# Two-model kernel: conv taps in portions of four and an output product that accumulates over both halves in shared PSUM banks

## The chip, the cores and the metric

The kernel runs on one core of a Trainium2 chip. The metric is device microseconds (us) of one execution; lower is better. The engines are called by the names of the profile: PE (TensorE, matmuls; PEld its weight loads), DVE (VectorE), ACT (ScalarE), POOL (GpSimd) and SP (SyncE, whose queue issues most transfers).

## The reference, cut to what matters

The program computes two models one after the other. The change touches the first one alone: two layers over 256 tokens of width 1024. Each layer projects a normed input to many pieces, mixes tokens in three ways (a causal depthwise convolution with 31 taps, a pooling mixer, sparse attention), gates each, and multiplies the three joined results by `w_out`.

```python
for i in range(DEPTH):                      # DEPTH = 2
    n = rmsnorm(h, norm_g[i])
    z = n @ w_in[i] + b_in[i]
    (c_val, c_glu, c_gate, p_in, p_gate, q, k, v, a_gate, qi, ki, wi) = jnp.split(z, cut, axis=-1)
    ya = conv_module(c_val, c_glu, ...) * jax.nn.silu(c_gate)   # 31 taps, layernorm, silu, 1x1
    yb = pool_mixer(p_in, ...) * jax.nn.silu(p_gate)
    yc = sparse_attention(q, k, v, qi, ki, wi) * jax.nn.silu(a_gate)
    h = h + jnp.concatenate([ya, yb, yc], axis=-1) @ w_out[i]
    h = h + (p[i] @ ple_w[i]) * jax.nn.sigmoid(h @ ple_gate_w[i])
return rmsnorm(h, final_norm_g)
```

## The kernel before

Activations lie transposed: 128 features on the partitions, 256 tokens along the row, so a tensor of width 1024 is eight tiles of 128x256. Each operand of a large product is split into a high and a low half (`split`, `unit`), and one product is three matmuls: high by high, high by low, low by high (`mm3`). A weight unit of 128x1024 is loaded by SP into `raw`, its high half is copied by ACT and its low half is a subtraction on DVE (`hl<-raw,hl`, line 449). In the notes below, "the split" of a weight unit is this subtraction. An output tile with all eight input tiles takes 24 matmuls (`mtile`).

A layer of the first model runs like this: the norm; the tiles for the convolution, indexer, q, k and v; then eight **gate tiles** (`silu` of the gates, 24 matmuls each, one weight unit each); then the output product with `w_out` in two halves `g = 0, 1`, each over four of its eight input tiles (`WO_ORDER`). Each half has eight output tiles of 12 matmuls, and each is added to `h` on DVE (128x256, called `x` in traces). In the second half `h` is split again for the next product. After that the side input's product and its gate follow.

Convolution, pooling, indexer and attention are generators (`conv1`, `pool1`, `index1`, `attn1`). They run in the shadow of the tiles: `tick(budget)` is called behind a tile and lets tasks issue until the costs that they yield have used up the budget (1500 where nothing is given). From the gates on the tasks take turns. `conv1` issues one `scalar_tensor_tensor` of 128x256 (`acc<-u,sp,acc`, stt for short) for each filter position and each of two channel halves, 60 in a layer; each of these instructions is called a tap here. It yields `CONVY` = 900 after every two of them. Behind the taps come its norm (`acc,o`, `csq`, `clr` in the trace) and its 1x1 product (`csq,sw`). Attention's matmuls are named `kr,qr`, `aL` (transposes) and `aPT,v`. `flush()` between the halves lets all tasks run out, since the second half's input tiles are the convolution's and the last heads' results.

The order within each engine is then settled by a scheduler, and all engines run their own stream in order. PSUM banks are handed out by tag: three for `mm`, four for `ax` (tasks), one for `ada`.

Of the kernel before, what the change touches and what calls it, by code (L numbers as in the profile page):

```python
# [12 lines left out]
ALU = mybir.AluOpType  # L13
# [4 lines left out]
T = 256  # L18
KT = 8
# [3 lines left out]
FIRST = 2  # L23
PAIR_PACE = 2.2
DOWN_PACE = 2.5
CONVY = 900
INNER = 650
INNER_K = (1, 3, 5)
R_TICK, NQ_TICK, SC_TICK = 650, 900, 1000
# [75 lines left out]
WO_ORDER = (2, 3, 4, 5, 6, 7, 0, 1)  # L105
# [247 lines left out]
class Prog:  # L353
# [209 lines left out]
        return ps  # L563


    def ftile(s, x, keep=False):
        w = s.raw0.pop(0) if s.raw0 else s.rawunit()
        ps = s.bank("mm")
        for k in range(KT):
            if keep:  # L570
                s.warm(KEEP, 256)
            s.mm(ps[:, :T], w[:, k * 128 : k * 128 + 128], x[:, k], k == 0, k == KT - 1)
        return ps
# [164 lines left out]
    def layer1(s, i):  # L738
# [9 lines left out]
        h = s.h  # L748
# [8 lines left out]
        gh = s.gh  # L757
        rs = s.t([128, T], "rs", 1)

        def norm():  # L760
            R = s.spread(s.rstd_cols(s.st[0]["ps"][:, 0:2], 2, 1.0 / D), 2)
            s.a(rs, R[:, :T], AF.Copy)
            for k in range(KT):
                n = s.t([128, T], "nf", 2, pool=s.sm)
                s.tt(n, gh[:, k], rs, ALU.mult)
                s.split(s.xx[:, 1, 0, k], s.xx[:, 1, 1, k], n)

        tile_no = [-1]
        raws = [s.ftile(gh, i == 0 and j == 0) for j in range(FIRST)]
        norm()  # L770

        def wtile():
            tile_no[0] += 1
            if tile_no[0] not in PLAIN:
                return s.mtile(T, T)
            ps = raws.pop(0) if raws else s.ftile(gh)
            y = s.t([128, T], "yc", 2)
            s.tt(y, ps[:, :T], rs, ALU.mult)
            return y
# [5 lines left out]
        def bias():  # L785
            j = bi[0]
            bi[0] += 1
            return P["b"][:, j : j + 1], H["b"][:, j : j + 1]
# [6 lines left out]
        for j in range(2):  # L795
            ps = wtile()
# [7 lines left out]
        for j in range(2):  # L804
            ps = wtile()
# [11 lines left out]
        ps = wtile()  # L817
# [5 lines left out]
        for tt in range(2):  # L823
            ps = s.bank("mm")
            for k in range(KT):
                o = (k % 3) * 260
# [4 lines left out]
        for j in range(2):  # L831
            ps = wtile()
# [10 lines left out]
        for nme in ("q", "k"):  # L843
            raw = s.t([128, 4, T], nme + "r", 1)
            for j in range(4):
                ps = wtile()
# [8 lines left out]
        for uu in range(4):  # L855
            hl = s.unit()
            for tt in range(2):
                for kk in range(2):
                    k = uu * 2 + kk
# [19 lines left out]
        for j in range(8):  # L879
            ps = s.mtile(T, T)  # L880
            b, hb = bias()
            zh = s.t([128, T], "zh", 2)
            th = s.t([128, T], "th", 2)
            s.a(th, ps[:, :T], AF.Tanh, bias=hb, scale=0.5)
            s.a(zh, ps[:, :T], AF.Identity, bias=hb, scale=0.5)
            s.stt(sil[:, j], th, 1.0, zh, ALU.add, ALU.mult)
            st8[GATES[j]] = sil[:, j]
            if i == DEPTH - 1 and j == RCTX:
                ps = s.spread(rc, 2)
                s.a(s.rctx, ps[:, :T], AF.Copy)  # L890
            s.tick()
        s.pace = PACE[3]
        s.pool_share = 0.0
        s.until(st8, "pool")
        s.until(st8, ("att", 1))


        for g in range(2):
            if g:
                s.turns = False  # L900
                s.flush()
            for m in range(KT):
                if m % 2 == 0:
                    hl = s.unit()
                ps = s.mtile(0, T, hl, WO_ORDER[4 * g : 4 * g + 4], m % 2 * 4)
                s.tt(h[:, m], h[:, m], ps[:, :T], ALU.add)
                if g:
                    s.split(s.xx[:, 1, 0, m], s.xx[:, 1, 1, m], h[:, m])
                s.tick()
        s.pace = PACE[4]  # L910
        if i < DEPTH - 1:
            s.spn = s.small1(i + 1)
# [10 lines left out]
        for m in range(KT):  # L923
            pe = s.bank()
            for k in range(2):
                o = (m % 4) * 256 + k * 128
# [3 lines left out]
            ps = s.mtile(T, T)  # L930
# [4 lines left out]
            e = nc.gpsimd if SQP[0] else None  # L935
            s.sumsq_add(st[0], h[:, m], 2, m == 0, m == KT - 1, eng=e)
            out, g = (h, P["fin"]) if lastl else (s.gh, s.spn["g"])
# [13 lines left out]
    def conv1(s, i, P, H, u, cat, st8):  # L951
        nc = s.nc
        acc = s.t([128, 2, T], "acc", 1)
        for j in range(2):
            s.ts(acc[:, j], u[:, j, 0:T], P["dw"][:, j * CONV_K : j * CONV_K + 1], ALU.mult,
                 P["dwb"][:, j : j + 1], ALU.add)
        for k in range(1, CONV_K):
            for j in range(2):
                s.stt(acc[:, j], u[:, j, k : k + T], P["dw"][:, j * CONV_K + k : j * CONV_K + k + 1], acc[:, j],
                      ALU.mult, ALU.add)  # L960
            yield CONVY
        while "late" not in st8:
            yield None
        o256 = s.t([128, 128], "o256", 1)
        s.ts(o256, s.ones, 1.0 / 256, ALU.mult)
        ps = s.bank()
        for j in range(2):
            s.mm(ps[:, :T], o256, acc[:, j], j == 0, j == 1)
        for j in range(2):
            s.tt(acc[:, j], acc[:, j], ps[:, :T], ALU.subtract)  # L970
        yield CSTEP
        sq = s.t([128, 2, T], "csq", 1)
        s.a(sq, acc, AF.Square)
        st = s.bank()
        for tt in range(2):
            for j in range(2):
                s.mm(st[:, tt : tt + 1], sq[:, j, tt * 128 : tt * 128 + 128], s.ones[:, 0:1], j == 0, j == 1)
        r = s.rstd_cols(st[:, 0:2], 2, 1.0 / 256, "cl")
        yield CSTEP
        R = s.spread(r, 2)  # L980
        for j in range(2):
            s.tt(acc[:, j], acc[:, j], R[:, :T], ALU.mult)
            th = s.t([128, T], "th", 2)
            s.a(th, acc[:, j], AF.Tanh, bias=H["lnb"][:, j : j + 1], scale=H["lng"][:, j : j + 1])
            s.a(sq[:, j], acc[:, j], AF.Identity, bias=H["lnb"][:, j : j + 1], scale=H["lng"][:, j : j + 1])
            s.stt(sq[:, j], th, 1.0, sq[:, j], ALU.add, ALU.mult)
            yield 700
        while ("c", 1) not in st8:
            yield None
        pw = P["pw"].rearrange("p (k f) -> p k f", k=2)  # L990
        for m in range(2):
            ps = s.bank()
            for j in range(2):
                s.mm(ps[:, :T], pw[:, j, m * 128 : m * 128 + 128], sq[:, j], j == 0, j == 1)
            s.stt(acc[:, m], ps[:, :T], P["pwb"][:, m : m + 1], st8["c", m], ALU.add, ALU.mult)
            s.split(cat[0][:, m], cat[1][:, m], acc[:, m])
            yield 700
        st8["conv"] = True
# [776 lines left out]
```

## Time and profile before

| What | Value |
|---|---|
| Time, median of 3 runs | 1443.52 us (1440.94 to 1445.94) |
| The profiled execution | 1444.92 us |
| Its span in the trace | 1443.1 us |
| Mean granted clock of TensorE | 0.98 |
| Busy: PE, DVE, ACT, POOL | 1388.4, 1134.6, 671.9, 68.4 us |

The profiled execution's time is a little more than its span, which runs from the first to the last event that the trace holds. Busy times overlap. The granted clock is the share of TensorE's full speed that it was given. In the traces an idle entry `[0.98 <-ACT xx L414]` says that the engine stood idle for 0.98 us before the instruction, and which instruction ended the wait.

### The profile page before, as it was taken

To read this page: it belongs to the slowest core of one execution; us is meant where nothing else is said; L and a number is where in the kernel's file an instruction comes from. 1 tells how busy PE (TensorE), PEld (TensorE's weight loads), DVE (VectorE), ACT (ScalarE), POOL (GpSimd) and SP (SyncE) were. 2 spreads that over 40 slices of the span, in tenths; PEclk is the share of its full clock that TensorE was granted. 3 is DMA by queue.
4 is the path that set the end of the run, shared out by engine and by line. 5 is a ranking of instruction groups with operands and counts; after the bars stand their busy time and mean duration, and the time that the engine had idled before them with its cause. 6 is when DMAs were issued, how large, how long until landed. Compare 5 with 4: busy or idle time off the path is not lost.

```text
span 1443.1 us, 25346 instructions
## 1 busy us (share of the span) xinstructions
PE 1388.4 (96%) x9914; PEld 1188.0 (82%) x9914; DVE 1134.6 (79%) x2430; ACT 671.9 (47%) x1234; POOL 68.4 (5%) x92
## 2 busy tenths in 40 slices
PE   8999899998999999998999999999899999999997
PEld 7878899788978777678888888888788887999997
DVE  6998679997879666897788877888678556798794
ACT  4446555465753241545443312443145346565562
POOL 0000000000200001003000000001200000100001
PEclk9999899998999998999999999999999999999998
DMA  7973356334543432332444564557732232366662
GB/s 263 330 250 118 103 170 201 125 104 130 194 148 116 132 100 73 117 114 89 133 144 132 160 191 146 174 177 251 229 115 89 89 97 88 116 212 197 183 198 74
DMA packets 63903, 219.03 MB, mean 152 GB/s; under 512 B 7270, under 2 KB 12328, under 8 KB 63528
## 3 DMA queue, kind: packets, MB, share of 16 engines
q1 hardware_dynamic: 58368, 209.22, 45.8%
q10 hardware_dynamic: 5416, 8.20, 1.7%
q8 instruction: 78, 1.28, 0.4%
q14 instruction: 41, 0.34, 0.1%
HBM read 216.34 MB, written 1.05 MB: 151 GB/s over the span
## 4 chain that ended last, share of the span: by engine, by line
PE 73%; DVE 11%; issue 6%; DMA 4%; ACT 3%; POOL 2%; ACTq 0%; POOLq 0%; DVEq 0%; SPq 0%
PE mm L388 20%; PE mm L389 20%; PE mm L390 19%; PE ax L385 9%; DVE hl L449 3%; DMA wada<-in_wadaT_dram 2%; PE mm L385 1%; DMA raw<-in_units_dram 1%; PE ax L1728 1%; PE ada L385 1%; POOL sqa L537 1%; DVE xx L396 1%; DVE wada L683 1%; DMA crow<-in_crow_dram 1%; ACT hl L441 1%
## 5 line engine op out<-in xcount | busy, mean ns | idle before, releaser
L388 PE MATMUL mm<-xx,hl 128*128 128x256 f32 (+1 forms) x1720 | 557.5, 326 | 5.5 <-ACT xx L414 2.0
L390 PE MATMUL mm<-xx,hl 128*128 128x256 f32 (+1 forms) x1720 | 547.1, 319 | 1.6 <-DVE hl L449 1.5
L389 PE MATMUL mm<-xx,hl 128*128 128x256 f32 (+1 forms) x1720 | 547.6, 319 | 0.0
L441 ACT ACTIVATE hl<-raw 128x1024 fp32r<-128x1024 f32 x286 | 301.3, 1055 | 186.8 <-PE mm L390 152.4
L449 DVE TENSOR_TENSOR hl<-raw,hl 128x1024 fp32r<-128x1024 f32 x286 | 348.9, 1221 | 49.3 <-ACT hl L441 47.6
L388 PEld LDWEIGHTS mm<-xx,hl 128*128 128x128 f32 x1720 | 325.6, 190 | 51.8 <-issue 17.9
L390 PEld LDWEIGHTS mm<-xx,hl 128*128 128x128 f32 x1720 | 325.9, 190 | 30.6 <-DVE hl L449 3.2
L389 PEld LDWEIGHTS mm<-xx,hl 128*128 128x128 f32 x1720 | 326.5, 190 | 28.4 <-issue 4.9
L396 DVE SCALAR_TENSOR_TENSOR y<-mm,sp,y 128x255 f32<-128x255 f32 (+1 forms) x184 | 109.0, 595 | 30.9 <-ACT y L409 29.6
L389 PE MATMUL mm<-hid,hl 128*128 128x256 f32 (+1 forms) x374 | 124.2, 332 | 0.0
L388 PE MATMUL mm<-hid,hl 128*128 128x256 f32 (+1 forms) x374 | 124.2, 332 | 0.0
L390 PE MATMUL mm<-hid,hl 128*128 128x256 f32 (+1 forms) x374 | 124.1, 332 | 0.0
L683 DVE CUSTOM_DVE_ANT_0 wada<-wada,crow,sp 128x1024 f32<-128x1024 f32 x80 | 102.9, 1292 | 13.6 <-DMA wada<-in_wadaT_dram 13.2
L409 ACT ACTIVATE y<-mm,sp 128x256 f32<-128x256 f32 (+1 forms) x92 | 60.5, 658 | 97.9 <-PE mm L390 97.8
L390 PEld LDWEIGHTS mm<-hid,hl 128*128 128x128 f32 x374 | 71.9, 192 | 7.1
L388 PEld LDWEIGHTS mm<-hid,hl 128*128 128x128 f32 x374 | 71.8, 192 | 7.1
L389 PEld LDWEIGHTS mm<-hid,hl 128*128 128x128 f32 x374 | 71.8, 192 | 7.1
L389 PE MATMUL mm<-hl,xx 128*128 128x416 f32 (+3 forms) x192 | 65.9, 346 | 2.5 <-DVE hl L449 2.5
L396 DVE SCALAR_TENSOR_TENSOR x<-mm,mod,x 128x256 f32<-128x256 f32 x96 | 43.6, 479 | 30.2 <-PE mm L390 30.1
L537 POOL TENSOR_TENSOR sqa<-sqa,sq 128x256 f32<-128x256 f32 x36 | 35.3, 987 | 675.7 <-ACT sq L409 674.8
L388 PE MATMUL mm<-hl,xx 128*128 128x416 f32 (+3 forms) x192 | 65.9, 349 | 0.2 <-ACT hl L441 0.2
L390 PE MATMUL mm<-hl,xx 128*128 128x416 f32 (+3 forms) x192 | 65.6, 344 | 0.0
(278 smaller groups left out, 1691.0 us busy)
## 6 DMA issues: line engine op xcount, KB each, us to landing
raw<-in_units_dram SPq DMA_DIRECT2D x296, 512.0 KB, 3.8
wada<-in_wadaT_dram SPq DMA_DIRECT2D x80, 512.0 KB, 3.5
wada<-in_wada_dram SPq DMA_DIRECT2D x16, 512.0 KB, 6.2
nab<-in_nab_dram ACTq DMA_DIRECT2D x12, 192.0 KB, 3.4
crow<-in_crow_dram SPq DMA_DIRECT2D x2, 1024.0 KB, 7.4
x<-in_xT_dram SPq DMA_DIRECT2D x4, 256.0 KB, 5.9
x<-in_ctxT_dram ACTq DMA_DIRECT2D x1, 1024.0 KB, 11.9
c<-in_c_dram ACTq DMA_DIRECT2D x1, 928.0 KB, 5.9
```

Of the source, the lines that this page charges most:

```text
L385: return s.nc.tensor.matmul(out, lhsT, rhs, start=start, stop=stop, **kw)
L388: s.nc.tensor.matmul(out, l[0], r[0], start=start, stop=False)
L389: s.nc.tensor.matmul(out, l[0], r[1], start=False, stop=False)
L390: s.nc.tensor.matmul(out, l[1], r[0], start=False, stop=stop)
L396: s.nc.vector.scalar_tensor_tensor(out, a, sc, b, op0, op1)
L409: s.nc.scalar.activation(out, in_, func, bias=bias, scale=scale)
L441: a = nc.scalar.activation(hl[:, 0], raw, AF.Copy)
L449: b = nc.vector.tensor_sub(hl[:, 1], raw, hl[:, 0].bitcast(F32))
L537: (eng or s.nc.vector).tensor_tensor(st["acc"], st["acc"], sq, ALU.add)
L683: s.pin(nc.vector.tensor_tensor_reduce(out=w, in0=w, in1=c[:, j], scale=1.0, scalar=bias[:, m : m + 1], op0=ALU.mult, op1=ALU.add, accum_o ...
L1728: nc.tensor.transpose(pt[:, kt * 128 : kt * 128 + 128], L[j][:, kt * 128 : kt * 128 + 128], s.ident)
```

## The change

Four edits, all in the first model. The taps are issued four at a time, and such a portion costs 1300. A gate tile's tick has a budget of 2800. The norm works on pairs of tiles (128x512). The output product keeps its sums in four PSUM banks (three `mm`, one `ada`) over both halves: a bank holds a pair of output tiles side by side, the first half (`g = 0`) only accumulates, and in the second half one addition of 128x2x256 and one split of 128x512 follow per pair. Ticks are left in the first half only. Lines behind the edits move by 1 to 18 (the split of weight units is line 450, the matmuls of the output product are line 386).

```diff
-CONVY = 900
+CONVY = 1300
+GATE_TICK = 2800
...
+    def part(s, out, hl, ks, off, g):
+        for q, k in enumerate(ks):
+            o = (q + off) * 128
+
+            s_, e_ = not g and not off and q == 0, bool(g) and bool(off) and q == len(ks) - 1
+            r = [s.mv(e, k, 0, T) for e in range(2)]
+            kw = dict(skip_group_check=True)
+            s.mm(out, hl[:, 0, o : o + 128], r[0], s_, False, **kw)
+            s.mm(out, hl[:, 0, o : o + 128], r[1], False, False, **kw)
+            s.mm(out, hl[:, 1, o : o + 128], r[0], False, e_, **kw)
...
-            for k in range(KT):
-                n = s.t([128, T], "nf", 2, pool=s.sm)
-                s.tt(n, gh[:, k], rs, ALU.mult)
-                s.split(s.xx[:, 1, 0, k], s.xx[:, 1, 1, k], n)
+            for k in range(0, KT, 2):
+                n = s.t([128, 2, T], "nh", 2)
+                s.tt(n, gh[:, k : k + 2], rs.unsqueeze(1).to_broadcast([128, 2, T]), ALU.mult)
+                s.split(s.xx[:, 1, 0, k : k + 2], s.xx[:, 1, 1, k : k + 2], n)
...
-            s.tick()
+            s.tick(GATE_TICK)
...
+        wo = [s.bank("mm" if b < 3 else "ada") for b in range(4)]
         for g in range(2):
             if g:
                 s.turns = False
                 s.flush()
-            for m in range(KT):
-                if m % 2 == 0:
-                    hl = s.unit()
-                ps = s.mtile(0, T, hl, WO_ORDER[4 * g : 4 * g + 4], m % 2 * 4)
-                s.tt(h[:, m], h[:, m], ps[:, :T], ALU.add)
+            for m in range(0, KT, 2):
+                hl, ps = s.unit(), wo[m // 2]
+                for d in range(2):
+                    s.part(ps[:, d * T : d * T + T], hl, WO_ORDER[4 * g : 4 * g + 4], d * 4, g)
+                    if not g:
+                        s.tick()
                 if g:
-                    s.split(s.xx[:, 1, 0, m], s.xx[:, 1, 1, m], h[:, m])
-                s.tick()
+                    hm = h[:, m : m + 2]
+                    s.tt(hm, hm, ps.rearrange("p (k t) -> p k t", k=2), ALU.add)
+                    s.split(s.xx[:, 1, 0, m : m + 2], s.xx[:, 1, 1, m : m + 2], hm)
...
-            yield CONVY
+            if k % 2 == 0:
+                yield CONVY
```

Three places show how the order on the engines moves, all in layer 0. The first is PE between the two halves of the output product before; `mm_1716`, `mm_1732` and `mm_1753` are tiles of the second half.

```order
L385 MATMUL ax_1662<-c_82,csq_1660 128x1 x4
L385 MATMUL ax_1671<-c_82,clr_1669 128x128 x2
L385 MATMUL ax_1684<-csq_1660,sw_102 128x256
L385 MATMUL ax_1690<-csq_1660,sw_102 128x256
L1104 MATMUL ax_1696<-c_82,aL_1593 128x128
L385 MATMUL ax_1684<-csq_1660,sw_102 128x256
L385 MATMUL ax_1690<-csq_1660,sw_102 128x256
L1104 MATMUL ax_1696<-c_82,aL_1593 128x128 x3
L385 MATMUL ax_1624<-aPT_1701,v_816 64x128 x4
L388 MATMUL mm_1716<-xx,hl_1713 128x256
L388 MATMUL mm_1732<-xx,hl_1713 128x256
L388 MATMUL mm_1753<-xx,hl_1750 128x256
```

After the change PE's stream at the end of the first half reads as follows; `mm_1534`, `mm_1535`, `mm_1536` and `ada_1537` are the four shared banks.

```order
L1122 MATMUL ax_1569<-c_82,aL_1529 128x128 x2
L386 MATMUL mm_1535<-xx,hl_1598 128x256
L1122 MATMUL ax_1569<-c_82,aL_1529 128x128 x2
L386 MATMUL mm_1535<-xx,hl_1598 128x256 x9
L386 MATMUL ax_1560<-aPT_1574,v_808 64x128 x4
L386 MATMUL mm_1535<-xx,hl_1598 128x256 x14
L386 MATMUL mm_1536<-xx,hl_1627 128x256 x24
L386 MATMUL ada_1537<-xx,hl_1656 128x256 x24
L386 MATMUL mm_1534<-xx,hl_1685 128x256 x24
L386 MATMUL mm_1535<-xx,hl_1717 128x256 x24
L386 MATMUL mm_1536<-xx,hl_1749 128x256 x24
L386 MATMUL ada_1537<-xx,hl_1781 128x256 x24
```

The last attention matmuls (`aPT`) and transposes (`aL`) stood between the halves and stand inside the first half now; 62 matmuls of the product lie between the last of them and the second half, and the conv norm's matmuls (`csq`, `clr`) have moved from here to the gate tiles.

The second place is DVE from the end of the v tiles to the split for a gate tile, before; `hl_1069` belongs to gate tile 3, `v_816` is the sum for v.

```order
L449 TENSOR_TENSOR hl_1069<-raw_1067,hl_1069 128x1024
L1052 MATCH_REPLACE iwk_757<-im_758,iwk_757 128x256
L405 TENSOR_TENSOR v_816<-mm_817,tokb_109 128x512
L1051 MAX im_758<-iwk_757 128x8
L405 TENSOR_TENSOR mod_452<-ax_930,sp_249 128x4x2
L1052 MATCH_REPLACE iwk_757<-im_758,iwk_757 128x256
L405 TENSOR_TENSOR mod_452<-ax_930,sp_249 128x4x2
L405 TENSOR_TENSOR imk_873<-iwk_757,isc_699 128x256
L405 TENSOR_TENSOR v_816<-mm_818,tokb_109 128x512
L402 TENSOR_SCALAR imk_873<-imk_873 128x256
L396 SCALAR_TENSOR_TENSOR acc_390<-u_206,sp_80,acc_390 128x256 x2
L449 TENSOR_TENSOR hl_1123<-raw_1121,hl_1123 128x1024
```

After the change the stretch that ends with the split for gate tile 1 (`hl_945`) reads like this.

```order
L397 SCALAR_TENSOR_TENSOR acc_374<-u_190,sp_80,acc_374 128x256
L1070 MATCH_REPLACE iwk_749<-im_750,iwk_749 128x256
L397 SCALAR_TENSOR_TENSOR acc_374<-u_190,sp_80,acc_374 128x256
L406 TENSOR_TENSOR imk_865<-iwk_749,isc_691 128x256
L397 SCALAR_TENSOR_TENSOR acc_374<-u_190,sp_80,acc_374 128x256
L403 TENSOR_SCALAR imk_865<-imk_865 128x256
L397 SCALAR_TENSOR_TENSOR acc_374<-u_190,sp_80,acc_374 128x256
L406 TENSOR_TENSOR mod_444<-ax_926,sp_233 128x4x2 x2
L397 SCALAR_TENSOR_TENSOR acc_374<-u_190,sp_80,acc_374 128x256 x4
L406 TENSOR_TENSOR v_808<-mm_809,tokb_109 128x512
L406 TENSOR_TENSOR v_808<-mm_810,tokb_109 128x512
L450 TENSOR_TENSOR hl_945<-raw_943,hl_945 128x1024
```

Before, the first gates' splits stood ahead of the additions to v, with few taps between; now eight taps and both additions to v come ahead of the first gate's split. By the split of gate tile 5, 28 of the layer's 60 taps have been issued before, and all 60 after, in either layer.

The third place is DVE in the second half of the output product, before.

```order
L405 TENSOR_TENSOR x_70<-x_70,mm_1716 128x256
L415 TENSOR_TENSOR xx<-x_70,xx 128x256
L405 TENSOR_TENSOR x_70<-x_70,mm_1732 128x256
L405 TENSOR_TENSOR x_70<-x_70,mm_1753 128x256
L449 TENSOR_TENSOR hl_1869<-raw_1867,hl_1869 128x1024
L415 TENSOR_TENSOR xx<-x_70,xx 128x256 x2
L405 TENSOR_TENSOR x_70<-x_70,mm_1769 128x256
L449 TENSOR_TENSOR hl_1874<-raw_1872,hl_1874 128x1024
```

And after.

```order
L406 TENSOR_TENSOR x_70<-x_70,mm_1534 128x2x256
L450 TENSOR_TENSOR hl_1821<-raw_1819,hl_1821 128x1024
L416 TENSOR_TENSOR xx<-x_70,xx 128x512
L406 TENSOR_TENSOR x_70<-x_70,mm_1535 128x2x256
L450 TENSOR_TENSOR hl_1826<-raw_1824,hl_1826 128x1024
L416 TENSOR_TENSOR xx<-x_70,xx 128x512
L406 TENSOR_TENSOR x_70<-x_70,mm_1536 128x2x256
L450 TENSOR_TENSOR hl_1841<-raw_1839,hl_1841 128x1024
```

Two additions of 128x256 with their two subtractions have become one of each of twice the width, and one weight split stands between an addition and its subtraction.

## Rows read from the trace of the kernel before

**Rows 1.** The page, part 1: span, then busy time of TensorE.
```profile
span 1443.1 us, 25346 instructions
...
PE 1388.4 (96%) x9914; PEld 1188.0 (82%) x9914; DVE 1134.6 (79%) x2430; ACT 671.9 (47%) x1234; POOL 68.4 (5%) x92
```

**Rows 2.** Windows: busy time in each stretch (instructions), clock, DMA share, GB/s.
```profile
core 0: us, PE busy (x) PEld busy (x) DVE busy (x) ACT busy (x) POOL busy (x), PEclk, DMA share, GB/s
60.00:100.00 40.00, 40.00 (x310) 30.07 (x306) 39.71 (x109) 18.05 (x34) 0.00 (x0) 1.00 0.87 305
...
140.00:160.00 20.00, 14.60 (x82) 12.67 (x82) 9.24 (x25) 6.65 (x12) 0.70 (x1) 0.74 0.16 52
...
200.00:280.00 80.00, 76.52 (x529) 68.01 (x527) 76.10 (x187) 41.51 (x77) 1.61 (x1) 1.00 0.54 177
...
320.00:340.00 20.00, 13.01 (x61) 10.60 (x62) 11.95 (x24) 4.96 (x11) 1.61 (x1) 0.74 0.33 106
```

**Rows 3.** Timeline of PE, layer 0, around the flush: start, duration, instruction, idle.
```profile
142.60 0.28 PE L390 MATMUL mm<-xx,hl 128*128 128x256 f32 x1
...
145.43 1.22 PE L385 MATMUL ax<-c,clr 128*128 128x128 f32 x4 [1.03 <-POOL clr L519]
148.82 2.07 PE L385 MATMUL ax<-csq,sw 128*128 128x256 f32 x4 [2.17 <-DVE csq L396]
...
153.45 0.66 PE L385 MATMUL ax<-aPT,v 128*64 128x128 f32 x8 [0.75 <-ACT aPT L409]
155.08 0.93 PE L388 MATMUL mm<-xx,hl 128*128 128x256 f32 x3 [0.98 <-ACT xx L414]
...
158.15 0.41 PE L389 MATMUL mm<-xx,hl 128*128 128x256 f32 x1
158.37 0.40 PE L390 MATMUL mm<-xx,hl 128*128 128x256 f32 x1
...
158.73 0.28 PE L389 MATMUL mm<-xx,hl 128*128 128x256 f32 x1
158.84 0.28 PE L390 MATMUL mm<-xx,hl 128*128 128x256 f32 x1
```

**Rows 4.** Timeline of PE, layer 1, around the flush.
```profile
325.82 1.21 PE L385 MATMUL ax<-c,clr 128*128 128x128 f32 x4 [1.72 <-POOL clr L519]
329.41 3.60 PE L385 MATMUL ax<-csq,sw 128*128 128x256 f32 x8 [2.38 <-DVE csq L396]
...
334.13 0.66 PE L385 MATMUL ax<-aPT,v 128*64 128x128 f32 x8 [0.69 <-ACT aPT L409]
335.77 0.75 PE L388 MATMUL mm<-xx,hl 128*128 128x256 f32 x3 [0.98 <-ACT xx L414]
...
339.40 0.34 PE L389 MATMUL mm<-xx,hl 128*128 128x256 f32 x1
```

**Rows 5.** Timeline of DVE, both layers: splits of gate tile 5, and taps in a row.
```profile
92.99 1.20 DVE L449 TENSOR_TENSOR hl<-raw,hl 128x1024 fp32r<-128x1024 f32 x1
...
121.49 2.05 DVE L396 SCALAR_TENSOR_TENSOR acc<-u,sp,acc 128x256 f32<-128x256 f32 x5
...
280.50 1.22 DVE L449 TENSOR_TENSOR hl<-raw,hl 128x1024 fp32r<-128x1024 f32 x1
```

**Rows 6.** Timeline of PE: first matmul of gate tile 5 in each layer.
```profile
106.25 0.39 PE L388 MATMUL mm<-xx,hl 128*128 128x256 f32 x1
...
284.33 0.38 PE L390 MATMUL mm<-xx,hl 128*128 128x256 f32 x1
```

**Rows 7.** Groups by form on DVE, 0 to 400 us: count, busy us, mean ns, idle before.
```profile
L396 DVE SCALAR_TENSOR_TENSOR acc<-u,sp,acc 128x256 f32<-128x256 f32 x120 | 53.1, 477 | 0.0
L405 DVE TENSOR_TENSOR x<-x,mm 128x256 f32<-128x256 f32 x32 | 12.8, 418 | 7.6 <-PE mm L390 7.3
...
L405 DVE TENSOR_TENSOR v<-mm,tokb 128x512 f32<-128x512 f32 x4 | 2.7, 688 | 0.0
```

**Rows 8.** Timeline of PE at the front of layer 0.
```profile
28.86 0.39 PE L389 MATMUL mm<-hl,xx 128*128 128x260 f32 x1 [1.17 <-DVE hl L449]
```

## Prediction

> **What bounds the kernel now.** I read the page first: TensorE is busy for 1388.4 of 1443.1 us, so the whole kernel can gain only where TensorE stands idle or runs slowly [rows 1]. The change touches the first model alone, the first 395 us or so; the windows over that part show where TensorE loses time. From 60 to 100 us it has no idle time at all and VectorE is busy for 39.71 of 40 us; in 140 to 160 it is busy for 14.60 of 20, and in 320 to 340 for 13.01, both at a mean granted clock of 0.74, while VectorE works for only 9.24 and 11.95 us there [rows 2]. These two stretches hold the flush of each layer. The timeline of PE shows what ends each wait. After the last matmul of g=0 at 142.60 TensorE waits in turn for POOL, VectorE and ScalarE: the norm of the convolution, then its 1x1 matmuls, then the last attention head. Only at 155.08 does g=1 begin, and its matmuls are 0.22 us apart until 158.37 and 0.11 us from 158.73 on [rows 3]. So the granted clock fell to its lower level (1.2 GHz) after that idle time and came back under the matmuls of g=1. Layer 1 has the same chain between 322 and 335.77 us [rows 4]. The reader is to see two things: both engines lack work in the flush, and the last tap of the convolution (inside g=0) is what came late.
>
> **The prices of the two flushes.** Layer 0: idle is 20 - 14.60 = 5.40 us [rows 2]. The slow stretch runs from about 148.8 to 158.58; less the 0.75 and 0.98 us of idle in it, TensorE works there for 8.0 us at half speed, which costs 4.0 [rows 3]. Together 9.4 us. Layer 1: idle 20 - 13.01 = 6.99 [rows 2]; slow from 329.41 to 339.5, less 0.69 and 0.98, is 8.4 us, costing 4.2 [rows 4]. Together 11.2 us. These are ceilings, 20.6 us in all, since the work itself stays.
>
> **Does the change remove these waits?** In the new order the conv norm's matmuls stand among gate tiles 5 to 8, and behind the last attention matmul of g=0 there are 62 matmuls of the output product. At 0.11 us each they last 6.9 us. What follows that last matmul before g=1 may start is short: before, the last attention matmuls began at 153.45, lasted 0.66, and g=1 waited 0.98 more [rows 3]. Even with one weight split of 1.2 us in front of it on VectorE [rows 5], the 6.9 us cover it. I take the flush stall as gone in both layers: -9.4 and -11.2.
>
> **What the taps cost in front of the gates.** The taps are not removed, only put earlier: 32 more of the 60 taps stand ahead of the split for gate tile 5, in each layer. Five in a row take 2.05 us [rows 5], so 0.39 each with the overlap, and 32 take 12.5. Some 15 further operations of attention and pool (0.34 us apart as the additions of [rows 7], or less) stand ahead in layer 0, 5.2 us; in layer 1 it is 6 or 7, or 2.2 us. A split that comes later holds up the gate tile's low half on TensorE, and behind it everything, since TensorE works in order.
> Layer 0: that split ended at 94.19 [rows 5] and TensorE wanted it at 106.25 [rows 6], a lead of 12.1 us. It now comes 17.7 us later. TensorE itself arrives later too, because it has more ahead of it (two conv norm matmuls, four attention pieces, pool, six early gate matmuls; about 3.5 us by the 0.11 to 0.35 us of such matmuls). 17.7 - 12.1 - 3.5 leaves 2.1 us. It is a cost of 2.0, between 0 (the sums of durations on both sides can be off by 2 us) and 5 (the next tiles can find their splits late as well).
> Layer 1: the split ended at 281.72 and TensorE was there at 284.33 [rows 5, 6], a lead of only 2.6 us, because VectorE is the bound before it: busy 76.10 of 80 us from 200 to 280 [rows 2]. 14.7 - 2.6 - 3.0 leaves 9.1 us; some 1 us of VectorE's waits ahead of it can be filled. I take 8.0, between 3 and 11.
> After gate tile 5 the debt shrinks, since VectorE has no taps left and the splits for g=0 come sooner than they are wanted.
>
> **VectorE's work itself.** 16 additions of 128x256 per layer (418 ns each) become four of 128x512 (688 ns, as the additions to v) [rows 7]. With the 0.08 us by which neighbours overlap (0.477 against 0.39 for a tap), this is 16 x 0.34 - 4 x 0.61 = 3.0 us less; 8 splits of the output into 4 save 0.3, norm by pairs 0.6. This 3.9 us lies where TensorE is the bound, mostly behind g=0, so I credit nothing (bounds 0 and -1.5 in layer 1).
>
> **Norm by pairs at the front.** Here TensorE waited 1.17 us for a split [rows 8]. The norm gets shorter by 0.6 but delays the first weight splits. I take -0.5, between -1.5 and +1.
>
> **A wait added by the shared banks.** An addition of a pair now starts after 24 matmuls, not 12, and behind it on VectorE stand a weight split and the subtraction. For the last pair: addition 0.61, weight split 1.13, subtraction 0.61, with ScalarE's copy beside the split: 2.4 us, up to 3.2 if ScalarE has a weight copy in front of it. The cover is 6 matmuls of the side input and 18 of the next product, 24 x 0.114 = 2.7 us. So 0 to 0.5, taken as 0.4 per layer, bounds 0 and 1.5. The banks being held for g=0 leaves the gate tiles' early matmuls to wait for one: 0.3 per layer, bounds 0 and 1.
> The Trainium skill ("PSUM — Partial Sum Buffer", the section on bank collisions) says that two engines must not touch one bank and quadrant at the same time and that the hardware neither arbitrates nor stalls. By it the first half of a pair can't be added while the second is being written, which speaks against sharing a bank. By the rule alone, with no cover, the two last subtractions would stand open: 2.4 us per layer. No row here shows it.
>
> **Loading and the second model.** On the DMA queue of SP the loads of raw weights stand in nearly the same order, some behind one more load of wada near 88 us; I take 0, bounds 0 and 1. The second model has the same instructions: 0, bounds -1.5 and +1.5.
>
> **Sum.** -9.4 + 2.0 - 11.2 + 8.0 - 0.5 + 2 x 0.4 + 2 x 0.3 = -9.7 us. The profiled execution took 1444.92 us, so 1435.2; the median of the three runs shown is 1.4 lower (1443.52), which gives about 1434.
>
> **The rivals.**
> *The gates cost next to nothing (24 in 100).* For it: VectorE idles for half of each flush [rows 2], so its work fits if the order lets it; my lateness hangs on sums over some 50 instructions, each of which can be off by 2 us or more. Then layer 0 pays 0 to 1 and layer 1 about 3: 1444.92 - 20.6 + 3.5 + 0.9 = 1428.7, or 1427 on the median.
> *VectorE becomes the bound in the gates (11 in 100, the side of a loss).* Place: gate tiles 1 to 6 of both layers. It decides when the waits there exceed 20.6 us, that is 10 us more than I allow. VectorE is already full in 60 to 100 and nearly so in 200 to 280 [rows 2]. If layer 0's lead were 9 us instead of 12.1 (17.7 - 9 - 3.5 = 5.2) and in layer 1 neither the lead nor TensorE's own delay helped beyond 1 us (14.7 - 1 = 13.7), 19 us would be paid, and a fall of the clock in the sparse gates would add half of some 10 us: 1444.92 - 20.6 + 19 + 5 + 0.9 = 1449, or 1448 on the median. Against it: TensorE idled for 3.48 us in 200 to 280 and the granted clock stayed at 1.00 [rows 2].
> The Trainium skill ("TensorE: Matmul & The Clock Gate", Part 1) says that throttled is the default state and that activity releases it. The fall in rows 3 and 4 agrees with it; by it alone a gate stretch with gaps as long as the flush's would run at 1.2 GHz, which is the 5 us of this rival.
> *The wait only moves (13 in 100, no change).* The last link of attention still comes after the end of g=0, or the wider pairs at the end of g=1 hold up the next product by 2.4 us a layer, and layer 1's gates pay all 11: about 1443. Against it stand the 62 matmuls.
>
> **How the numbers follow.** The forecast has 52 in 100. Its own range: best -9.4 + 0 - 11.2 + 3 - 1.5 - 1.5 = -20, worst -9.4 + 5 - 11.2 + 11 + 1 + 3 + 2 = +1, but not all together: 1428 to 1440. The range takes in most of the two nearer rivals: 1424 to 1443. A change under 0.3% (4.3 us) can't be told from none. The forecast lies 9.7 under, so nearly all of it and the first rival count as faster (0.75); the rest of it and the third rival as the same (0.15); the second rival as slower (0.10).
>
> **What would show it.** Right: in the changed profile the windows of the two flushes hold 19 to 20 us of TensorE work at a clock of 1.00; g=1 begins without an idle entry of a microsecond; about 2 us of waits for the splits in layer 0's gates and about 8 in layer 1's. Wrong: a granted clock under 1 between the gates, waits of over 15 us for splits in them, an idle entry between the end of g=1 and the next product, or g=1 still waiting for ScalarE's copy.

## The result, and the profile after

The changed kernel takes 1432.28 us (median of 6 runs, 1427.24 to 1435.14) against 1444.73 us before (6 runs, 1440.94 to 1447.32): a ratio of 0.9911 with a 95% interval of 0.9888 to 0.9934. The forecast was 1434, in a range of 1424 to 1443. The time came where it was forecast; the working behind it holds in part only, as the profile and the runs below show.

The page of the changed kernel, part 1:

```profile
span 1430.9 us, 25285 instructions
...
PE 1383.7 (97%) x9914; PEld 1181.7 (83%) x9914; DVE 1126.2 (79%) x2382; ACT 668.5 (47%) x1218; POOL 68.2 (5%) x92
```

Its windows over the stretches of [rows 2] and two more (columns as there):

```profile
80.00:100.00 20.00, 19.11 (x148) 13.26 (x147) 18.92 (x55) 7.15 (x18) 0.00 (x0) 1.00 0.57 204
100.00:120.00 20.00, 18.92 (x134) 14.73 (x133) 18.39 (x46) 13.14 (x33) 0.15 (x1) 1.00 0.32 85
...
140.00:160.00 20.00, 19.99 (x178) 19.61 (x178) 12.10 (x16) 9.84 (x12) 0.00 (x0) 1.00 0.47 139
...
240.00:260.00 20.00, 16.79 (x101) 13.04 (x100) 20.00 (x61) 6.45 (x10) 0.00 (x0) 1.00 0.34 107
260.00:280.00 20.00, 16.59 (x76) 12.90 (x74) 17.61 (x47) 6.61 (x16) 1.61 (x1) 0.74 0.30 102
280.00:300.00 20.00, 18.83 (x135) 14.73 (x133) 18.34 (x45) 13.05 (x33) 0.00 (x0) 1.00 0.32 86
...
320.00:340.00 20.00, 19.96 (x179) 19.59 (x178) 12.44 (x16) 9.89 (x12) 0.00 (x0) 1.00 0.57 176
```

Both flushes are full: 19.99 and 19.96 us of TensorE work at a granted clock of 1.00, where [rows 2] had 14.60 and 13.01 at 0.74. The idle time has moved ahead: 2.0 us in 80 to 120, and 7.8 us in 240 to 300, with the granted clock at 0.74 in 260 to 280.

The timeline of PE of the changed kernel at the end of layer 0's output product, the place of [rows 3]:

```profile
142.33 0.66 PE L386 MATMUL ax<-aPT,v 128*64 128x128 f32 x8
142.91 4.59 PE L386 MATMUL mm<-xx,hl 128*128 128x256 f32 x38
147.34 2.88 PE L386 MATMUL ada<-xx,hl 128*128 128x256 f32 x24
150.06 8.32 PE L386 MATMUL mm<-xx,hl 128*128 128x256 f32 x72
158.22 2.88 PE L386 MATMUL ada<-xx,hl 128*128 128x256 f32 x24
160.94 0.28 PE L389 MATMUL ax<-qi,hl 128*128 128x256 f32 x1
```

No row has an idle entry. The 62 matmuls (38 and 24) run from the last attention matmul to 150.06, and the second half starts there, 5.0 us before its old start.

The timeline of PE in layer 1, in the last two v units and at gate tile 1:

```profile
258.68 0.50 PE L390 MATMUL mm<-hl,xx 128*128 128x512 f32 x1 [1.46 <-DVE hl L450]
...
264.64 0.50 PE L390 MATMUL mm<-hl,xx 128*128 128x512 f32 x1 [2.93 <-DVE hl L450]
...
265.44 0.39 PE L390 MATMUL mm<-hl,xx 128*128 128x512 f32 x1
265.67 0.39 PE L391 MATMUL mm<-hl,xx 128*128 128x512 f32 x1
...
266.64 0.63 PE L389 MATMUL mm<-hl,xx 128*128 128x512 f32 x1
267.07 0.63 PE L390 MATMUL mm<-hl,xx 128*128 128x512 f32 x1
...
268.50 0.55 PE L389 MATMUL mm<-xx,hl 128*128 128x256 f32 x1 [0.37 <-DVE v L406]
```

and that of DVE there:

```profile
257.42 1.21 DVE L450 TENSOR_TENSOR hl<-raw,hl 128x1024 fp32r<-128x1024 f32 x1
...
263.36 1.23 DVE L450 TENSOR_TENSOR hl<-raw,hl 128x1024 fp32r<-128x1024 f32 x1
264.49 3.26 DVE L397 SCALAR_TENSOR_TENSOR acc<-u,sp,acc 128x256 f32<-128x256 f32 x8
267.66 1.29 DVE L406 TENSOR_TENSOR v<-mm,tokb 128x512 f32<-128x512 f32 x2
268.92 1.22 DVE L450 TENSOR_TENSOR hl<-raw,hl 128x1024 fp32r<-128x1024 f32 x1
```

TensorE waits for the splits of v, not first for those of the gate tiles. DVE has no gap. The split at 263.36 comes behind taps, and eight more taps follow in a row before the additions to v and gate tile 1's split. After these waits TensorE's matmuls of 128x512 are 0.23 us apart until 265.67 and 0.43 from 266.64: it fell to its lower level here, a good microsecond after the longer wait had ended. The window of the slow stretch:

```profile
266.00:276.30 10.30, 9.93 (x36) 7.64 (x36) 8.44 (x21) 2.31 (x6) 1.61 (x1) 0.50 0.32 103
```

**How the runs are compared below.** Single runs of one kernel differ by several us, so the experiments are read by three lengths within each profile. *Start* is the end of the 16th weight split on DVE (the last unit of v but one, layer 0). *L0* is from there to the first matmul of layer 0's side input (160.94 above). *L1* is from there to layer 1's. *Second* is from there to the end of the last weight split.

The ratios are to the runs of the kernel before on the same chip; the medians come from several chips. One of norm_only's ten runs took 4618.30 us, counts as slow and is left out.

| Kernel | Start | L0 | L1 | Second | Median us (runs) | Ratio, 95% interval |
|---|---|---|---|---|---|---|
| before | 75.0 | 91.7 | 180.8 | 1076.2 | 1444.73 (6) | |
| before_again | 74.4 | 93.7 | 181.3 | 1070.6 | 1440.69 (1) | |
| before_third | 75.1 | 89.7 | 182.5 | 1071.6 | 1439.70 (1) | |
| the changed kernel | 74.6 | 86.3 | 179.6 | 1070.9 | 1432.28 (6) | 0.9911, 0.9888 to 0.9934 |
| after_again | 73.3 | 86.9 | 178.1 | 1066.2 | 1425.23 (1) | |
| out_only | 75.3 | 90.6 | 177.5 | 1076.1 | 1440.61 (10) | 0.9982, 0.9963 to 1.0000 |
| portions_only | 74.2 | 87.1 | 176.7 | 1070.2 | 1432.67 (10) | 0.9937, 0.9913 to 0.9961 |
| norm_only | 75.5 | 94.3 | 181.9 | 1074.0 | 1445.33 (9) | 1.0012, 0.9981 to 1.0044 |
| portion2 | 76.2 | 87.7 | 172.7 | 1069.5 | 1429.18 (4) | 0.9920, 0.9888 to 0.9951 |
| gate1500 | 77.5 | 86.2 | 178.4 | 1075.8 | 1434.30 (6) | 0.9934, 0.9908 to 0.9961 |
| mix | 74.7 | 86.5 | 173.7 | 1070.1 | 1424.99 (4) | 0.9869, 0.9842 to 0.9895 |
| p2gate4k | 75.7 | 86.0 | 172.9 | 1078.0 | 1427.59 (4) | 0.9894, 0.9863 to 0.9925 |
| mixl | 75.4 | 86.2 | 178.1 | 1070.2 | 1432.69 (6) | 0.9921, 0.9896 to 0.9947 |
| mix_nobanks | 73.9 | 86.9 | 178.1 | 1071.6 | 1431.23 (5) | 0.9926, 0.9903 to 0.9949 |

### The profile page after: what moved, and what is told of

It reads as the page before. It is cut to its first block, busy times and chain, and to the rows that moved or that the text cites. A ratio compares the mean times of both kernels' runs of the same rounds, so it can differ in the third digit from the quotient of the medians.

```text
span 1430.9 us, 25285 instructions
## 1 busy us (share of the span) xinstructions
PE 1383.7 (97%) x9914; PEld 1181.7 (83%) x9914; DVE 1126.2 (79%) x2382; ACT 668.5 (47%) x1218; POOL 68.2 (5%) x92
## 4 chain that ended last, share of the span: by engine, by line
PE 75%; DVE 12%; DMA 5%; ACT 3%; issue 3%; POOL 2%; ACTq 0%; POOLq 0%; DVEq 0%; SPq 0%
PE mm L389 20%; PE mm L391 19%; PE mm L390 19%; PE ax L386 10%; PE mm L386 4%; DVE hl L450 3%; DMA wada<-in_wadaT_dram 2%; DMA raw<-in_units_dram 1%; PE ada L386 1%; DVE acc L397 1%; ACT hl L442 1%; PE ax L1746 1%; POOL sqa L538 1%; DVE wada L696 1%; DVE xx L397 1%
## 5 line engine op out<-in xcount | busy, mean ns | idle before, releaser
L389 PE MATMUL mm<-xx,hl 128*128 128x256 f32 (+1 forms) x1592 | 520.3, 328 | 4.8 <-ACT hl L442 2.4
L391 PE MATMUL mm<-xx,hl 128*128 128x256 f32 (+1 forms) x1592 | 511.9, 322 | 1.5 <-DVE hl L450 1.4
L390 PE MATMUL mm<-xx,hl 128*128 128x256 f32 (+1 forms) x1592 | 510.8, 322 | 0.3 <-DVE xx L416 0.2
L389 PEld LDWEIGHTS mm<-xx,hl 128*128 128x128 f32 x1592 | 301.4, 190 | 50.9 <-issue 18.5
L391 PEld LDWEIGHTS mm<-xx,hl 128*128 128x128 f32 x1592 | 301.8, 190 | 31.9 <-issue 3.1
L390 PEld LDWEIGHTS mm<-xx,hl 128*128 128x128 f32 x1592 | 302.1, 190 | 27.7 <-issue 4.1
L696 DVE CUSTOM_DVE_ANT_0 wada<-wada,crow,sp 128x1024 f32<-128x1024 f32 x80 | 103.4, 1298 | 12.4 <-DMA wada<-in_wadaT_dram 12.0
```

The lines of the kernel that those rows point to most:

```text
L389: s.nc.tensor.matmul(out, l[0], r[0], start=start, stop=False)
L390: s.nc.tensor.matmul(out, l[0], r[1], start=False, stop=False)
L391: s.nc.tensor.matmul(out, l[1], r[0], start=False, stop=stop)
L696: s.pin(nc.vector.tensor_tensor_reduce(out=w, in0=w, in1=c[:, j], scale=1.0, scalar=bias[:, m : m + 1], op0=ALU.mult, op1=ALU.add, accum_o ...
```

## The experiments

The theory (A) was: the taps in large portions move work out of the two flushes, and the changed kernel pays for it where weight splits come late on VectorE. The rivals were that the shared banks make the gain, and that what layer 1 lost was chance.

**The edits one by one.** out_only takes the changed kernel and undoes all but the output product:

```diff
-CONVY = 1300
+CONVY = 900
...
-            s.tick(GATE_TICK)
+            s.tick()
...
-            if k % 2 == 0:
-                yield CONVY
+            yield CONVY
```

and the norm tile by tile, as before.

> Of the four edits only the output product in shared banks. The conv norm and the last attention matmuls stay behind the first half (12 matmuls of the second half can slip ahead of the last of them). Theory A (the portions of taps empty the flush, the banks do not): the side input's product of layer 0 starts at 166 us (166.66 before, 160.94 in the changed kernel), that of layer 1 at 346 to 347 (347.41 and 340.52), the granted clock still falls in both flushes, and the time is within 3 us of before. Theory B (the shared banks let the second half be ready early): 162 and 342, 6 us or more faster.

portions_only is the opposite: the kernel before, with the three edits that this cut takes back and nothing else.

> Of the four edits only the portions of four taps and the budget of 2800 at gate tiles. Theory A: both flush waits go as in the changed kernel and the waits for splits in v and the gates come as there; the side input's product starts at 161 to 162 us in layer 0 and at 341 to 344 in layer 1; 5 to 11 us faster than before, 0 to 4 slower than the changed kernel. Theory B: flush waits remain (166 and 347) and the time is that of before.

norm_only is the kernel before with the norm by pairs.

> Of the four edits only the norm by pairs. Either theory: the front gains 0.4 us, layer 1's norm 0.3; 165.5 to 166.7 and 346 to 347.4 for the two products; time within 3 us of before. If the front mattered more than I think, it would be 2 us or more at the first product.

The windows of the two flushes, out_only first:

```profile
140.00:160.00 20.00, 15.12 (x89) 13.20 (x88) 7.73 (x19) 6.15 (x11) 0.70 (x1) 0.83 0.16 53
...
320.00:340.00 20.00, 14.83 (x91) 12.99 (x90) 9.61 (x20) 6.86 (x12) 0.87 (x1) 0.83 0.20 71
```

and portions_only:

```profile
140.00:160.00 20.00, 19.98 (x173) 19.61 (x173) 14.62 (x27) 9.80 (x15) 0.00 (x0) 1.00 0.46 136
240.00:280.00 40.00, 35.09 (x196) 26.64 (x195) 39.72 (x114) 14.95 (x32) 1.61 (x1) 0.91 0.32 105
320.00:340.00 20.00, 20.00 (x179) 19.91 (x176) 16.21 (x31) 10.77 (x18) 0.00 (x0) 1.00 0.55 171
```

The portions alone fill both flushes and bring the idle time of 240 to 280 us with them (4.9 us); the banks alone leave the flush waits. Theory A holds for layer 0: 166 was expected of out_only and 165.89 came, 161 to 162 of portions_only and 161.27 came. In layer 1 out_only reached its side product at 343.41, where I had expected 346 to 347 and the rival 342; so the banks alone do save some 3 to 5 us there (L1 177.5 against 180.8 to 182.5). portions_only reached it at 338.00, 3 us ahead of the 341 to 344 that I had expected. By time the portions alone can't be told from the whole change (ratios 0.9937 and 0.9911, whose intervals overlap), and the other two edits alone are within 0.2% of before. norm_only's products came at 169.76 and 351.64, later than expected; it too has slow stretches that the kernel before had not in its first profile (granted clock 0.93 in 160 to 180, 0.91 in 260 to 280). The three profiles of the kernel before differ by 4.0 us in L0 alone, so this says nothing against the norm; its time is that of before.

**The size of a portion.** portion2 is the changed kernel with `CONVY = 900` and a yield after each pair of taps; the budget of 2800 stays.

> The changed kernel with the taps two at a time at a cost of 900, as before, and the budget of 2800 at gate tiles kept. No taps move ahead of the last v split and fewer ahead of the gates; 30 matmuls instead of 62 cover the end of attention. Theory A (what the changed kernel loses, it loses at splits that come late): layer 0's product starts at 157 to 160 us, layer 1's at 333 to 338, time 2 to 7 us below the changed kernel. Rival (the loss is elsewhere, and taps come too late again): 161 to 165 and 341 to 346, time equal to the changed kernel or slower.

Layer 1 came as expected (172.7 us, 336.55 absolute), layer 0 did not: 163.90, against 157 to 160 expected. The timeline of PE in portion2, second half of layer 0's product, shows why:

```profile
148.92 1.10 PE L386 MATMUL ax<-c,clr 128*128 128x128 f32 x4 [1.37 <-POOL clr L520]
...
155.62 0.62 PE L386 MATMUL mm<-xx,hl 128*128 128x256 f32 x3 [0.59 <-ACT xx L415]
```

The taps end so late that the conv norm is back between the halves and its chain through POOL and ScalarE stands open again. So two taps at a time are right for layer 1 and a little late for layer 0, where L0 is 0.8 to 1.4 us longer than in the two profiles of the changed kernel.

**Portions by layer.** mix gives each layer what it bears:

```diff
-            if k % 2 == 0:
+            if i:
+                yield 900
+            elif k % 2 == 0:
                 yield CONVY
```

> The changed kernel with portions of four taps in layer 0 alone; layer 1 issues two at a time at 900, as in portion2. Theory A (layer 0 has room for taps ahead of its v tiles and gates, layer 1 has none): the side input's product starts at 160.5 to 161.5 us in layer 0 as in the changed kernel and at 332 to 335 in layer 1 (160.94 + the 172.65 that portion2 needs between the two); idle of TensorE from 240 to 280 under 4.5 us instead of 6.6; time 5 to 8 us below the changed kernel. Rival (what layer 1 lost came from a chance fall of the clock): 339 to 341, no difference.

Both layers came as expected: 161.21 and 334.87. The windows of mix:

```profile
240.00:260.00 20.00, 18.79 (x105) 15.10 (x103) 20.00 (x61) 6.44 (x11) 0.00 (x0) 0.91 0.38 125
260.00:280.00 20.00, 17.98 (x124) 14.67 (x124) 17.38 (x42) 11.64 (x26) 1.61 (x1) 1.00 0.35 109
280.00:300.00 20.00, 19.35 (x154) 16.16 (x153) 18.22 (x53) 14.71 (x40) 0.00 (x0) 1.00 0.34 106
```

Idle from 240 to 280 is 3.2 us where the changed kernel had 6.6, and the v waits of 1.46 and 2.93 are gone. L1 is 4.5 to 5.9 us shorter than in the two profiles of the changed kernel. So splits that come late were the loss, not chance; whether it has to be those of v, mixl asks below. mix's median of 1424.99 is the lowest of all; but a single run of the changed kernel on the same chip took 1425.23 (after_again), with the shortest second model of all. The first model is faster by the profiles; by how much the whole is, stays open within a few us.

**More budget at the gates, and less.** p2gate4k has portion2's taps and `GATE_TICK = 3700`; gate1500 has the changed kernel's taps and the old budget of 1500.

> Portions of two taps at 900 in both layers, and the budget at gate tiles 3700 instead of 2800. Taps ahead of gate tile 5's split: 38 and 40 of a layer, against 62 and 64 in the changed kernel and 34 and 36 in portion2; matmuls behind the last attention matmul and ahead of the side input's product: 156 and 168, against 158 and 158, and 126 and 125. Theory A: portion2's waits in the second half of the product go (2 us in layer 0, 1.5 in layer 1) and the splits still come in time: 158 to 161 and 329 to 333; 6 to 12 us below the changed kernel. Rival: the budget of 3700 brings back the late splits, 161 to 165 and 337 to 341, no gain.

> The changed kernel with the budget at gate tiles back at 1500. Portions of four are kept, so the taps ahead of v and of gate tile 1 stay as they are; only 11 or 12 matmuls cover the end of attention. Theory A (the budget moves the conv norm and attention out of the flush): waits of some 4 to 7 us come back behind g=0, 163 to 167 and 342 to 347; 2 to 8 us slower than the changed kernel. Rival (the portions alone empty the flush): as the changed kernel within 2 us.

p2gate4k is shorter than portion2 in layer 0 (86.0 against 87.7) and not in layer 1 (172.9 against 172.7). Its products came at 161.68, in the rival's range and 0.7 us beyond that of theory A, and at 334.62, between the two and 1.6 us from A's; its time is 4.7 us below the changed kernel's by the medians, where A had 6 to 12 and the rival no gain. (The tap counts in its expectation hold the layer's opening instructions too and are 2 and 4 too high.) gate1500 went to the rival: L0 86.2 and L1 178.4 are those of the changed kernel, and its later absolute times come from its start (77.5). Its timeline of PE at the end of layer 0's first half:

```profile
150.35 0.66 PE L386 MATMUL ax<-aPT,v 128*64 128x128 f32 x8
150.94 1.56 PE L386 MATMUL ada<-xx,hl 128*128 128x256 f32 x11
152.34 5.93 PE L386 MATMUL mm<-xx,hl 128*128 128x256 f32 x49
```

Eleven matmuls (1.4 us) instead of 62 cover the last attention matmul, and the second half starts without an idle entry. The budget at the gates was not needed; the earlier taps were.

**Is the second model part of the gain?** It is the same code in both kernels, yet it took 5.3 us less in the first pair of profiles. So both kernels were profiled again.

> The changed kernel once more, for a second profile. The first model is expected to give 160.9 and 340.5 us again within 0.5, since its order is fixed. The second model, which the change does not touch, took 5.3 us less in the changed profile than in that of before, 3 of them in 400 to 420 us, where only before had a granted clock below 1. If that is chance, the second model's length differs between the two profiles of one kernel by 2 us or more; if it is an effect of the change, it repeats within 0.5.

> The kernel before once more. Its first model should repeat: the time from the split for the last v unit but one of layer 0 to the side input's product of layer 0 91.7 us, and from there to that of layer 1 180.75, each within 1.5. The second model took 1076.2 us in the first profile (from layer 1's product to the last weight split), and 1070.9 and 1066.2 in the two profiles of the changed kernel. If its length is chance, this profile can lie anywhere from 1066 to 1078; if the change shortens it, it lies at 1074 to 1078 again.

> A third profile of the kernel before, for the same question: 1074 to 1078 us of second model if the change shortens it, anywhere from 1066 to 1078 if it is chance.

The kernel before gave 1076.2, 1070.6 and 1071.6 us, the changed one 1070.9 and 1066.2. One kernel differs from itself by 5.6 and 4.7 us, so the first difference is within chance. Over all fourteen profiles the second model ranges from 1066.2 to 1078.0 us, and the longest is that of a kernel with the shared banks (p2gate4k). The first models did not repeat as closely as I had expected either: after_again's products came at 160.15 and 338.28, not within 0.5 us of 160.9 and 340.5, and before_again's L0 is 2.0 us above 91.7, where I had allowed 1.5. In 400 to 420 us the first profile of before has

```profile
400.00:420.00 20.00, 20.00 (x66) 13.53 (x67) 11.69 (x23) 10.00 (x12) 0.00 (x0) 0.83 0.35 120
```

and before_again

```profile
400.00:420.00 20.00, 19.91 (x80) 13.84 (x79) 13.62 (x26) 10.82 (x13) 0.00 (x0) 1.00 0.42 142
```

The same part of the program ran once partly at the lower clock, once not.

**Four taps in layer 1's gates alone, and mix without the banks.** mixl is mix with portions of four in layer 1 from the gates on (`if i and "late" not in st8: yield 900`). mix_nobanks has mix's portions on the kernel before, without banks and norm by pairs (what the latter is worth, norm_only does not resolve).

> As mix, but layer 1 issues two taps at a time only up to the end of its v tiles and four at a time from the gates on. Theory A says that VectorE has room at the gates as soon as v is out of the way: the waits of 2 us around layer 1's conv norm (320 to 326 us in mix) shrink, the gates lose less than 1 us; layer 1 takes 171.5 to 173.5 us from product to product (173.7 in mix) and the time is that of mix within 2 us. Rival: late splits at the gates are as dear as at v, 176 us or more and 2 to 5 us slower than mix.

> The kernel before with mix's portions alone (four taps in layer 0, two in layer 1, budget 2800 at the gates); norm tile by tile and the output product without shared banks, as before. Theory A (the order of the taps is nearly all of the gain; the 3.9 us of VectorE work per layer that the wider operations save lie where TensorE is the bound): 86 to 88 us from the start mark to layer 0's side product, 172.5 to 175.5 from there to layer 1's, and the time of mix within 2 us. Rival (the saved VectorE work counts where splits are late): 176 to 179 in layer 1, and 3 to 6 us slower than mix.

Both went to the rival, at 178.1 us in layer 1; by the medians they lie 7.7 and 6.2 us above mix, more than the rivals had (2 to 5, and 3 to 6). In mixl the timeline of PE has the wait in a gate tile now:

```profile
287.92 0.38 PE L391 MATMUL mm<-xx,hl 128*128 128x256 f32 x1 [1.74 <-DVE hl L450]
```

Its granted clock is 0.83 in 280 to 300 (1.00 in mix). From 240 to 300 it idles for 5.9 us where mix idles for 3.9, from 300 to 340 for 0.0 where mix has 1.6; so most of its 4.4 us in L1 is the lower clock. In mix_nobanks the flush is back:

```profile
322.13 0.71 PE L386 MATMUL ax<-c,clr 128*128 128x128 f32 x4 [1.14 <-POOL clr L520]
325.10 3.75 PE L386 MATMUL ax<-csq,sw 128*128 128x256 f32 x8 [2.26 <-DVE csq L397]
```

The same place in mix:

```profile
320.69 0.71 PE L386 MATMUL ax<-c,clr 128*128 128x128 f32 x4 [0.52 <-POOL clr L520]
321.16 1.42 PE L386 MATMUL mm<-xx,hl 128*128 128x256 f32 x10
322.42 0.87 PE L386 MATMUL ada<-xx,hl 128*128 128x256 f32 x6
323.68 2.02 PE L386 MATMUL ax<-csq,sw 128*128 128x256 f32 x8 [0.39 <-DVE csq L397]
```

With two taps at a time the last ones stand in the first half of the output product. There the old output product also has eight additions on DVE, the shared banks have none. Without the banks the conv norm's spread (`clr`) comes 1.4 us later (322.13 against 320.69 in mix), and TensorE has less to fill the waits with: between `clr` and `csq,sw` it has 16 matmuls of the product in mix and none in mix_nobanks. It works for 16.43 us at 0.83 in 320 to 340, in mix for 18.48 at 1.00. In sum the banks are worth 4.4 us of L1 here.

## Why the prediction was right, and where it was not

**The flush prices.** Right, and shown: both stretches hold full work at full clock, in the changed kernel and with the portions alone. The slow stretch before was not one from 148.8 on, as I read it: the clock was 1.00 again between 151.8 and 155.2 us, and TensorE worked for 7.6 us at the lower level, not 8.0, which changes the price by 0.2. The reason given for the cover (62 matmuls) was more than needed; gate1500 does it with 11.

**Layer 0: -9.4 + 2.0 + 0.4 + 0.3 = -6.7.** Measured by L0: -5.1 (means of 91.7 and 86.6; -5.3 in the first pair). The idle in 80 to 120 us is 1.97, forecast 2.0. The remaining 1.6 us is within what L0 differs between profiles of the kernel before (4.0), and not settled. The price of the flush itself differs there: L0 of 89.7, 91.7 and 93.7 goes with a granted clock of 0.83, 0.74 and 0.67 in 140 to 160 us.

**Layer 1: -11.2 + 8.0 + 0.7 = -2.5.** Measured: -2.7 (181.5 and 178.9; -1.2 in the first pair). The term of 8.0 has about the right size: idle from 240 to 300 us rose from 2.9 to 7.8, and the slow stretch costs half of the 9.9 us that TensorE works in it, 5.0; together 9.9, inside the bounds of 3 and 11. With -11.2 this makes -1.3, as in the first pair. But half of it is the lower clock, which the term did not hold, and the step that placed it failed. I had set it at "the split for gate tile 5", reckoning 14.7 - 2.6 - 3.0 from there. The profile shows the waits earlier, in the v units and, 0.37 us, at gate tile 1, where the portions of four had already put more taps ahead (20, 28 and 36 of the layer's 60 stand ahead of the splits of the third and fourth v unit and of gate tile 1, against 12, 16 and 20 before). At gate tile 5 TensorE, late itself by then, waits 0.40 us:

```profile
295.19 0.38 PE L391 MATMUL mm<-xx,hl 128*128 128x256 f32 x1 [0.40 <-DVE hl L450]
```

Four taps in the gates are dear as well (mixl), so the mechanism, splits behind taps, is that of the forecast; its first place was v. Beside the banks the portions of four gain nothing in layer 1 by these profiles: out_only has 177.5 there, the changed kernel 179.6 and 178.1.

**The fall of the clock in the gates.** I gave it to the rival in which VectorE becomes the bound, and named a clock under 1 between the gates as a sign of being wrong. It came (0.74 in 260 to 280; 0.83 to 0.92 in the other profiles with portions of four in layer 1, and 0.91 in one window of mix too), at a cost of some 3 to 5 us by the same working, and without that rival's loss. The sentence that the clock stayed at 1.00 from 200 to 280 was true of before only. There the longest waits for a split were those of a v unit and of gate tile 4, 0.76 and 1.12 us; now it is 2.93:

```profile
258.89 0.50 PE L389 MATMUL mm<-hl,xx 128*128 128x512 f32 x1 [0.76 <-DVE hl L449]
...
279.45 0.39 PE L390 MATMUL mm<-xx,hl 128*128 128x256 f32 x1 [1.12 <-DVE hl L449]
```

**VectorE's work, "I credit nothing".** For the changed kernel nothing speaks against that: portions_only, without the saving, can't be told from it. As a rule it is wrong: where taps are left in the first half of the product, the shared banks are worth some 4 us of layer 1 (out_only against before; mix against mix_nobanks). Whether the additions that they spare do this, or the matmuls of the product that TensorE can run inside the conv norm's chain, no run separates.

**Norm by pairs, -0.5.** Not resolved: the start is 74.0 against 74.8 in the means, but 75.5 in norm_only.

**Tail and banks.** Forecast 0.4 per layer for the wider last pair. The first tile of layer 0's next product (24 matmuls) takes 3.21 us (161.65 to 164.86 in the timeline), where before took 2.90 (167.37 to 170.27) and portions_only, without the banks, 2.94: so 0.3. In layer 1 other matmuls stand in this tile, and it was not read there. The 0.3 for held banks was not measured by itself.

The Trainium skill ("PSUM — Partial Sum Buffer", the section on bank collisions) says that the hardware does not arbitrate where two engines touch one bank, which spoke against sharing one; no run here tests that rule. Without cover the prediction had 2.4 us per layer open at the end of the product. The 0.3 us above is what is left open in layer 0, so the cover holds there.

**The second model, 0 between -1.5 and +1.5.** The bounds were too narrow: single profiles of one kernel differ by 5 us there. This also bounds what the whole result says. Of the 12.4 us between the medians L0 and L1 explain 7.8 (5.1 and 2.7) and the start at most 0.9 (74.8 and 74.0, means whose profiles differ by as much); a further gain in the second model by the medians is neither shown nor excluded. The forecast of 9.7 us was all for the first model, where the profiles show 7.8 to 8.7, so it was 1 to 2 too high there, and its nearness to the measured time is partly luck. (The ends of its own range add up to -20.6 and +1.4, not -20 and +1; nothing hangs on that.)

## What to carry to other kernels

Work that must be done before a join belongs ahead of it only where the engine that does it has a lead: measure the lead of its splits, layer by layer, for every consumer from the point where the order starts to differ, and not at one tile. The same portion can be right in one layer and dear in the next (mix), so one constant for both leaves time behind in layer 1, even if the time of the whole kernel does not settle it here. Where two edits shorten the same chain (early taps, shared banks), one alone may do all of the work: in layer 0 the portions did it alone, and in layer 1 the banks alone came as far as both together.

## What the runs showed of the hardware that was not expected

The granted clock of the second model's stretches differs from run to run of one kernel: 0.83 and 1.00 in 400 to 420 us for the same part of the program. The second model's length differs by up to 5.6 us between the profiles of the kernel before, and the clock is not all of that: before_third is 4.6 us shorter there than the first profile, at a mean clock of 0.98 against 0.99. In the first model TensorE fell to 1.2 GHz after waits of 1.46 and 2.93 us a few us apart (0.43 us between 128x512 matmuls instead of 0.23), and in mixl after one of 1.74 (0.83 in 280 to 300), not only after the flush's longer chain of waits.
